# A hybrid decoder step: where the old states of the recurrent stage are scaled, who takes the first convolution tap, how masks and gates are formed

## The chip, the cores and the metric

The kernel runs on one core of a Trainium2 chip. A core has five engines that run their own instruction streams: TensorE (PE, matmuls; its weight loads are PEld), VectorE (DVE), ScalarE (ACT), GpSimd (POOL) and SyncE (SP, which issues DMAs here). They meet through semaphores. The metric is the device time of one execution in microseconds (us), lower is better.

## The reference

One layer of a decoder for 256 prompt tokens and 8 sequences of 8 sampled tokens (320 columns in all), width 2048. One projection feeds two branches. Branch A is a gated delta rule with 16 key heads and 32 value heads of 128 x 128 state; branch B is sparse attention. The part around the change:

```python
def causal_short_conv(x, buf, w):                       # 4 taps, then silu
    xp = jnp.concatenate([buf.astype(x.dtype), x], axis=1)
    y = sum(xp[:, i:i + L] * w[i] for i in range(CONV_W))
    return jax.nn.silu(y), xp[:, xp.shape[1] - (CONV_W - 1):]

decay = jnp.exp(jnp.where(incl, G[..., :, None] - G[..., None, :], -jnp.inf))
def chunk_step(s, xs):                                  # gated delta rule, one chunk
    u = u_c - jnp.einsum('bhck,bhkv->bhcv', w_c, s)
    o = jnp.einsum('bhck,bhkv->bhcv', qd_c, s) + jnp.einsum('bhij,bhjv->bhiv', qk_c, u)
    s = s * gt_c[..., None, None] + jnp.einsum('bhck,bhcv->bhkv', kt_c, u)

y = rms_norm(o, gdn_norm_g) * jax.nn.silu(z)            # the gates z
```

Everything is float32 at the edges.

## The kernel before

The big projections are a stream of weight blocks. Each unit is 1024 rows of 128 columns: SP loads it into `raw`, ACT rounds it into `whi`, DVE subtracts to get the rest `wlo` (the split), and PE multiplies both with the activations `xh`, `xl` into one of two PSUM banks `pm`: 8 pairs with `whi`, then 8 with `wlo`. `raw`, `whi` and `wlo` have three buffers each, so the split runs two units ahead.

All other work is written as Python generators ("sides") that are stepped between the pieces of the stream. A planner, the class `Clock`, keeps an estimated time for each engine from a cost formula (`cost`), and a side yields the time at which it wants to go on, for instance `self.ready(X)`. So the order of every engine's queue is fixed when the program is built; on the chip an instruction waits in that queue for what it needs. `force` steps sides until a buffer is free, whatever the planner's times.

The recurrent stage takes the projections of branch A, in eight groups of two key heads and four value heads (`gdn_chunks`). For each block of 128 channels `conv` copies the PSUM result to `xp` on ACT, forms four taps into the PSUM bank `u` (there is one such bank, a ring `cu`; rows name it ps), takes a tanh into `cth` on ACT, and DVE gates it into `kq`, `R` or `vf`. `z_done` forms the gates z (stored to `d_z`). `gb_gen` loads cumulated log decays into `gbt` (128 x 2 x 384), adds a mask of 0 and -1e30 and takes exponentials. `kq_gen` builds the matrices BT; `inverse` inverts them: 31 steps of two POOL instructions on `X` and `tmpx`, framed by DVE transposes of 32 x 32 blocks, then small matmuls that begin with `ps<-X,BD`. With the inverse XT in hand, `prompt_chain` and `sample_chain` run matmuls whose results DVE and ACT scale into `w` and `vt`. In `sample_chain`, S is the state of 8 sequences x 2 value heads (128 x 2048); its update S = S * gtr + k^T w reads four PSUM banks. `norm_gen` normalises the outputs `ot` (squares and their sums on ACT, `sc` holds the statistics, POOL takes the power -1/2), multiplies them with z and stores them to `d_ya`.

When all groups are through, the stream goes on with the remaining merge gates, `w_pb`, `w_pa` and `w_out`; `pb_open`, behind the second block of `w_pb`, first lets all normalisations end, and then loads gates (`sgb`).

Every instruction goes through the wrapper `Engine.__getattr__`, so the profile shows line L64 for all of them; groups are told apart by the names of their tiles.

Of the kernel before, what the change touches and what calls it, by code (L numbers as in the profile page):

```python
# [205 lines left out]
class Kernel:  # L206
# [260 lines left out]
    def consts(self):  # L467
        nc, f = self.nc, self.fix
        g, v = nc.gpsimd, nc.vector
        ji = self.l0.tile([128, 128], I32, name="ji")  # L470
# [8 lines left out]
        self.mask = self.l0.tile([128, 256], F32, name="mask")
        v.memset(self.mask, 0.0)  # L480
        self.select(self.mask)
        self.feat = f.tile([128, 81], F32, name="feat")
        self.gatp = f.tile([128, KB, 9], F32, name="gatp")

    def select(self, m):
        g = self.nc.gpsimd
# [2116 lines left out]
```

## Time and profile before

| | before |
|---|---|
| median of 3 runs | 2138.3 us (2138.07 to 2139.27) |
| profiled execution | 2140.89 us, its span 2139.2 us |
| mean granted TensorE clock | 0.994 |
| recurrent stage | about 728 to 1600 us of the span |
| HBM | 380.78 MB read, 42.65 MB written |

A row of groups reads: line, engine, operation, output <- inputs, shapes, xcount | busy us, mean ns of one | idle us of the engine before them <- who ended it. A row of the timeline reads: start, us, engine, line, operation, what, xcount, and in brackets the idle time before it and who ended that. PE's matmuls overlap, so the mean of one is longer than the step from one to the next.

### The profile page before, as it was taken

The page shows a single profiled execution, that of the slowest core. Times are in us where ns is not written, and L with a number is a line of the kernel's source. Part 1 is how long each engine was busy: PE and PEld are TensorE (multiplying, and loading weights), DVE is VectorE, ACT ScalarE, POOL GpSimd, SP SyncE. Part 2 cuts the span into 40 slices and gives each one's busy share as a digit, 9 for nine tenths or more (in the row PEclk, how much of TensorE's full clock was granted, in tenths as well). Part 3 has the DMA queues.
Part 4 walks back from the last instruction along what each step waited for, and adds up shares of the span by engine and source line. Part 5 has one row for each costly group of instructions (what it writes and reads, how often), then busy time and mean ns, then how long its engine had stood idle before and what let it go on. Part 6 is the DMA issues. An engine that isn't in the chain of part 4 may idle for free.

```text
span 2139.2 us, 44986 instructions
## 1 busy us (share of the span) xinstructions
PE 2093.5 (98%) x17741; PEld 2024.0 (95%) x17741; DVE 1462.1 (68%) x2881; ACT 1005.1 (47%) x2290; POOL 491.6 (23%) x713
## 2 busy tenths in 40 slices
PE   7999999999999999999999999999999999999997
PEld 7999999999999999898989998999999999999997
DVE  4776648899845577888778788778867445445443
ACT  4225443333434456565756565666556334233343
POOL 1001000000010128094636084508550000000000
PEclk9999999999999999999999999999999999999998
DMA  9996659885686757575757684758488767555562
GB/s 346 334 336 184 192 148 262 244 253 139 200 274 187 223 157 191 149 213 151 209 154 207 166 220 129 200 156 225 131 217 249 221 200 214 167 157 144 166 178 84
DMA packets 658595, 426.69 MB, mean 199 GB/s; under 512 B 19568, under 2 KB 642896, under 8 KB 656080
## 3 DMA queue, kind: packets, MB, share of 16 engines
q1 hardware_dynamic: 654304, 401.17, 65.8%
q0 software_dynamic: 3616, 21.02, 2.7%
q8 instruction: 139, 2.28, 0.4%
q10 hardware_dynamic: 464, 1.65, 0.2%
q14 instruction: 72, 0.59, 0.1%
HBM read 380.78 MB, written 42.65 MB: 198 GB/s over the span
## 4 chain that ended last, share of the span: by engine, by line
issue 24%; PE 19%; DVE 9%; POOL 5%; ACT 2%; DMA 1%; DVEq 0%; SPq 0%; POOLq 0%; ACTq 0%
PE pm L64 14%; PE ps L64 5%; POOL X L64 2%; POOL tmpx L64 2%; DVE wlo L64 2%; DVE S L64 2%; DVE ps L64 1%; DVE blk L64 1%; ACT ot L64 1%; POOL sc L64 1%; DVE X L64 0%; ACT whi L64 0%; DVE w L64 0%; DVE sc L64 0%; DVE BT L64 0%
## 5 line engine op out<-in xcount | busy, mean ns | idle before, releaser
L64 PE MATMUL pm<-xh,whi 128*128 128x320 f32 (+1 forms) x3108 | 942.1, 317 | 5.9 <-ACT whi L64 4.4
L64 PE MATMUL pm<-xl,whi 128*128 128x320 f32 (+1 forms) x3108 | 912.2, 308 | 0.4 <-DVE xl L64 0.3
L64 DVE TENSOR_TENSOR wlo<-raw,whi 128x1024 fp32r<-128x1024 f32 x466 | 580.3, 1254 | 247.2 <-ACT whi L64 225.9
L64 PEld LDWEIGHTS pm<-xh,whi 128*128 128x128 f32 x3108 | 586.4, 189 | 28.7 <-issue 18.0
L64 PEld LDWEIGHTS pm<-xl,whi 128*128 128x128 f32 x3108 | 586.8, 189 | 1.5 <-DVE xl L64 0.8
L64 ACT ACTIVATE whi<-raw 128x1024 fp32r<-128x1024 f32 x466 | 489.4, 1059 | 175.0 <-PE pm L64 115.8
L64 PE MATMUL pm<-xh,wlo 128*128 128x320 f32 (+1 forms) x3108 | 521.8, 307 | 3.6 <-DVE wlo L64 3.5
L64 PEld LDWEIGHTS pm<-xh,wlo 128*128 128x128 f32 x3108 | 469.2, 188 | 5.4 <-DVE wlo L64 5.3
L64 POOL TENSOR_TENSOR X<-X,tmpx 128x31 f32<-128x31 f32 (+15 forms) x248 | 180.6, 728 | 19.4
L64 POOL TENSOR_TENSOR tmpx<-blk,X 128x31 f32<-128x31 f32 (+15 forms) x248 | 168.9, 681 | 18.4
L64 DVE SCALAR_TENSOR_TENSOR ps<-xp,cs,ps 128x344 f32<-128x344 f32 x192 | 111.5, 581 | 6.8
L64 POOL TENSOR_TENSOR rfin<-rfin,mh 128x3 f32<-128x3 f32 x1 | 0.8, 848 | 485.9 <-DVE rfin L64 485.9
L64 PE MATMUL pm<-y1h,whi 128*128 128x320 f32 x336 | 99.2, 308 | 0.0
L64 PE MATMUL pm<-y1l,whi 128*128 128x320 f32 x336 | 99.1, 307 | 0.0
L64 POOL TENSOR_TENSOR sc<-sc,mh 128x6 f32<-128x6 f32 (+1 forms) x24 | 43.5, 1813 | 229.4 <-DVE sc L64 178.5
L64 POOL DMA_INDIRECT a<-in_cache_k_dram,idx x8 | 7.5, 937 | 283.1 <-PE ps L64 268.1
L64 DVE SCALAR_TENSOR_TENSOR S<-S,gtr,ps 128x128 f32<-128x128 f32 x256 | 67.5, 346 | 0.1
L64 ACT ACTIVATE xp<-pm 128x256 f32<-128x256 f32 (+1 forms) x128 | 32.0, 304 | 70.5 <-PE pm L64 70.5
L64 PE MATMUL ps<-xh,whi 128*128 128x320 f32 (+1 forms) x220 | 64.7, 309 | 0.0
L64 PE MATMUL ps<-xl,whi 128*128 128x320 f32 (+1 forms) x220 | 63.6, 304 | 0.0
L64 PEld LDWEIGHTS pm<-y1l,whi 128*128 128x128 f32 x336 | 63.1, 188 | 0.0
L64 PEld LDWEIGHTS pm<-y1h,whi 128*128 128x128 f32 x336 | 62.8, 187 | 0.0
(426 smaller groups left out, 2883.7 us busy)
## 6 DMA issues: line engine op xcount, KB each, us to landing
raw<-in_w_in_dram SPq DMA_DIRECT2D x328, 512.0 KB
raw<-in_w_pa_dram SPq DMA_DIRECT2D x64, 512.0 KB
rawx<-in_w_ada_dram SPq DMA_DIRECT2D x18, 1024.0 KB
a<-in_w_ada_dram SPq DMA_DIRECT2D x16, 1024.0 KB
S<-in_state_gdn_dram SPq DMA_DIRECT2D x32, 512.0 KB
out_dram<-S SPq DMA_DIRECT2D x32, 512.0 KB
raw<-in_w_pb_dram SPq DMA_DIRECT2D x32, 512.0 KB
raw<-in_w_out_dram SPq DMA_DIRECT2D x32, 512.0 KB
```

The source lines that it names most:

```text
L64: made = fn(*args, **kw)
```

## The change

Nine edits, all but the first three in the stage above:

- the planner's costs: a transpose of 3-dimensional pieces 0.2 + 0.0019 us an element (before, the general 0.16 + 0.00106), an `affine_select` 0.3 + 0.0009;
- the mask builder `select` is written into `consts`, and the stage's `mask3` goes;
- the four early gates (`z_early`) change as `z_done` does;
- conv: the first tap is an ACT copy with a scale;
- gates: z = (tanh + 1) * p in one DVE instruction straight from the bank; the factor `gh` is applied in `norm_gen`;
- decay masks: five `affine_select` on POOL for each key head in place of the DVE addition;
- inverse: the BD matmuls are placed 1.5 us after X is ready by the planner;
- chains: `w` for two heads in one instruction; S is scaled by POOL after its last read, and DVE adds one bank (512 elements) at a time;
- norm: two statistics steps merged, one on POOL; the scaling of `ot` is placed 1.5 us after its factors are ready by the planner.

```diff
@@ cost
+            if op == "transpose" and len(outs[0].ap) > 2:
+                return 0.2 + n * 0.0019
...
-        if op == "memset":
-            return 0.1 + n * 0.0009
+        if op in ("memset", "affine_select"):
+            return (0.1 if op == "memset" else 0.3) + n * 0.0009
@@ conv
-        self.ts(u[:, 0:344], xp[:, 0:344], wv(0), None, OP.mult)
+        self.act(u[:, 0:344], xp[:, 0:344], AF.Copy, scale=wv(0))
@@ z_done
-        self.force(lambda: self.zf.free and self.cth.free)
-        z, t = self.zf.get(), self.cth.get()
-        self.act(z, p[:, :NT], AF.Copy, scale=self.gh)
-        self.act(t[:, :NT], p[:, :NT], AF.Tanh, scale=0.5)
-        self.stt(z, t[:, :NT], 1.0, z, OP.add, OP.mult)
-        self.cth.put(t)
+        self.force(lambda: self.zf.free)
+        z = self.zf.get()
+        self.act(z, p[:, :NT], AF.Tanh, scale=0.5)
+        self.stt(z, z, 1.0, p[:, :NT], OP.add, OP.mult)
@@ gb_gen
-        self.tt(gb, gb, self.mask3.rearrange("p (o i) -> p o i", o=1).to_broadcast([128, 2, 384]), OP.add)
+        self.emitted += 1
+        g = gb[:, :, 0:256].rearrange("p v (t i) -> p v t i", t=2)
+        nc.gpsimd.affine_select(g, g, pattern=[[0, 2], [0, 2], [1, 128]], compare_op=OP.is_ge, fill=NEG, base=0,
+                                channel_multiplier=-1)
+        for v in range(2):
+            g = gb[:, v, 256:384].rearrange("p (b q) -> p b q", b=8)
+            nc.gpsimd.affine_select(g, g, pattern=[[-16, 8], [0, 16]], ...)
+            g = gb[:, v, 256:384].rearrange("p (b q t) -> p b q t", b=8, q=2)
+            nc.gpsimd.affine_select(g, g, pattern=[[16, 8], [0, 2], [1, 8]], ...)
@@ inverse, ahead of the BD matmuls
-        yield
+        yield self.ready(X) + 1.5
@@ prompt_chain (twice) and sample_chain
-        for v in range(2):
-            self.ts(wt[:, v, :], p[:, 128 * v:128 * v + 128], stl(v, 0), None, OP.mult)
+        self.tt(wt, p[:, 0:256].rearrange("p (v d) -> p v d", v=2), stl(0), OP.mult)
@@ sample_chain
         self.R.put(R)
+        self.tt(S, S, self.gtr[:, :, hv:hv + 2].rearrange("p b (v o) -> p b v o", o=1).to_broadcast([128, NB, 2, 128]),
+                OP.mult, eng=nc.gpsimd)
...
         yield
+        yield self.ready(S)
         yield from self.need(self.ps_side, 4)
...
         for j in range(4):
-            for pp in range(2):
-                for v in range(2):
-                    bb = 2 * j + pp
-                    self.stt(S[:, bb, v, :], S[:, bb, v, :], self.gtr[:, bb, hv + v:hv + v + 1],
-                             ps[j][:, 256 * pp + 128 * v:256 * pp + 128 * v + 128], OP.mult, OP.add)
+            sj = S[:, 2 * j:2 * j + 2].rearrange("p b v d -> p (b v d)")
+            self.tt(sj, ps[j], sj, OP.add)
@@ norm_gen
-        self.tt(mv(6), mv(6), qf, OP.mult)
-        self.ts(m[:, 6:12], m[:, 6:12], 1.0 / 128, EPS, OP.mult, OP.add)
+        self.stt(mv(6), mv(6), 1.0 / 128, qf, OP.mult, OP.mult)
+        self.ts(m[:, 6:12], m[:, 6:12], EPS, None, OP.add, eng=nc.gpsimd)
...
         self.tt(mv(12), mv(12), qf, OP.mult)
+        yield self.ready(m) + 1.5
         for t in range(3):
...
-            self.tt(y[:, 0:NP], p[:, 0:NP], z[:, 0:NP], OP.mult)
+            self.stt(y[:, 0:NP], p[:, 0:NP], self.gh, z[:, 0:NP], OP.mult, OP.mult)
```

Since the planner's times change, the order of all queues in the stage changes with them. Three places follow; a number behind a name is that of a buffer.

DVE, the third state update (h = 2, buffer S_7862). Before:

```order
L64 TENSOR_TENSOR wlo_82<-raw_75,whi_79 128x1024
L64 STREAM_TRANSPOSE blk<-X 128x32x32
L64 SCALAR_TENSOR_TENSOR vt_7851<-ps_71,neG,vt_7851 128x128 x2
L64 SCALAR_TENSOR_TENSOR vf_7831<-cth_7814,ps_68 128x256
L64 SCALAR_TENSOR_TENSOR vf_7831<-cth_7814,ps_68 128x8x8
L64 SCALAR_TENSOR_TENSOR S_7862<-S_7862,gtr,ps_70 128x128 x4
L64 SCALAR_TENSOR_TENSOR S_7862<-S_7862,gtr,ps_69 128x128 x4
L64 SCALAR_TENSOR_TENSOR S_7862<-S_7862,gtr,ps_67 128x128 x4
L64 SCALAR_TENSOR_TENSOR S_7862<-S_7862,gtr,ps_72 128x128 x4
L64 TENSOR_TENSOR wlo_83<-raw_75,whi_80 128x1024
```

Now on DVE (the buffer is S_7857, the conv bank u is ps_68):

```order
L64 TENSOR_TENSOR wlo_81<-raw_77,whi_78 128x1024
L64 SCALAR_TENSOR_TENSOR w_7850<-w_7850,gtp,ps_71 128x128 x2
L64 TENSOR_TENSOR ot_7856<-ps_71,ot_7856 128x256
L64 TENSOR_TENSOR S_7857<-ps_70,S_7857 128x512
L64 TENSOR_TENSOR S_7857<-ps_67,S_7857 128x512
L64 TENSOR_TENSOR S_7857<-ps_69,S_7857 128x512
L64 TENSOR_TENSOR S_7857<-ps_72,S_7857 128x512
L64 COPY ct_7812<-xp_7808 128x27
L64 SCALAR_TENSOR_TENSOR ps_68<-xp_7808,cs_95,ps_68 128x344 x3
```

and on POOL, where the same group's two scalings stand around the start of the next inverse (the memset and copies of X):

```order
L64 TENSOR_TENSOR X<-X,tmpx 128x31
L64 TENSOR_TENSOR sc_7862<-sc_7862,mh 128x10
L64 MEMSET X 32x4x32 x3
L64 COPY X<-X 32x4x32 x2
L64 COPY XT_7843<-blk 32x12x32 x2
L64 TENSOR_TENSOR S_7857<-S_7857,gtr 128x2048
L64 MEMSET X 128x640
L64 COPY X<-BT_7834 32x384 x2
L64 COPY BO<-BT_7834 64x256
L64 TENSOR_TENSOR S_7858<-S_7858,gtr 128x2048
```

Sixteen DVE instructions become four, and the multiplication is a POOL instruction behind the old inverse.

ACT, at the fifth normalisation. Before, its scaling `ot<-ot,sc` stands right behind a conv's copies and ahead of two weight copies:

```order
L64 ACTIVATE cth_7814<-ps_68 128x344
L64 ACTIVATE xp_7812<-pm_66 128x256
L64 ACTIVATE xp_7812<-pm_66 128x8x8
L64 ACTIVATE xp_7812<-cs_96 128x8x3
L64 ACTIVATE ot_7860<-ot_7860,sc_7867 128x128 x6
L64 ACTIVATE whi_79<-raw_75 128x1024
L64 ACTIVATE whi_80<-raw_75 128x1024
```

Now, with the tap behind the conv's copies (`ps_68<-xp,cs`), two weight copies behind the tap, and the scaling behind these:

```order
L64 ACTIVATE whi_80<-raw_75 128x1024
L64 ACTIVATE xp_7809<-pm_65 128x256
L64 ACTIVATE xp_7809<-pm_65 128x8x8
L64 ACTIVATE xp_7809<-cs_96 128x8x3
L64 ACTIVATE ps_68<-xp_7809,cs_96 128x344
L64 ACTIVATE whi_78<-raw_76 128x1024
L64 ACTIVATE whi_79<-raw_76 128x1024
L64 ACTIVATE cth_7810<-ps_68 128x344
L64 ACTIVATE ot_7855<-ot_7855,sc_7861 128x128 x6
```

DVE, where `w_pb` begins to be merged (`M<-pm,sgb`). Before, the last gates of the stage (`zf`) were over long before; the rows ahead of M were splits alone:

```order
L64 TENSOR_TENSOR wlo_81<-raw_76,whi_78 128x1024
L64 TENSOR_TENSOR wlo_82<-raw_76,whi_79 128x1024
L64 TENSOR_TENSOR wlo_83<-raw_77,whi_80 128x1024
L64 TENSOR_TENSOR wlo_81<-raw_77,whi_78 128x1024
L64 TENSOR_TENSOR M<-pm_66,sgb 128x320
L64 TENSOR_TENSOR M<-pm_65,sgb 128x320
```

Now the last four gates stand directly ahead of it:

```order
L64 TENSOR_TENSOR wlo_81<-raw_77,whi_78 128x1024
L64 SCALAR_TENSOR_TENSOR zf_7829<-ps_69,gh,zf_7829 128x256
L64 SCALAR_TENSOR_TENSOR zf_7829<-ps_69,gh,zf_7829 128x64
L64 SCALAR_TENSOR_TENSOR zf_7830<-ps_67,gh,zf_7830 128x256
L64 SCALAR_TENSOR_TENSOR zf_7830<-ps_67,gh,zf_7830 128x64
L64 TENSOR_TENSOR M<-pm_66,sgb 128x320
L64 TENSOR_TENSOR M<-pm_65,sgb 128x320
```

On PE the eight BD steps stand, counted in weight matmuls from the start, at 4236, 4860, 5304, 5844, 6528, 6960, 7632, 8016 before and at 4296, 4812, 5316, 5832, 6552, 7056, 7512, 8196 now; `w_pb` begins at 8448 in both.

More of the change, by code (lines that the diff above doesn't have):

```diff
@@ L480, in consts @@
         v.memset(self.mask, 0.0)
[L481 to L486, printed above, removed]
+        m = self.mask
         g.affine_select(m[:, 0:128], m[:, 0:128], pattern=[[1, 128]], compare_op=OP.is_ge, fill=NEG, base=0,
@@ L493, in select @@
                         channel_multiplier=-1)
+        self.feat = f.tile([128, 81], F32, name="feat")
+        self.gatp = f.tile([128, KB, 9], F32, name="gatp")
     def startup(self):
@@ L1319, in z_early @@
     def z_early(self, p, h):
-        self.force(lambda: len(self.t_r.free) >= 2)
-        z, t = self.t_r.get(), self.t_r.get()
-        self.act(z, p[:, :NT], AF.Copy, scale=self.gh)
-        self.act(t, p[:, :NT], AF.Tanh, scale=0.5)
-        self.stt(z, t, 1.0, z, OP.add, OP.mult)
-        self.t_r.put(t)
+        self.force(lambda: self.t_r.free)
+        z = self.t_r.get()
+        self.act(z, p[:, :NT], AF.Tanh, scale=0.5)
+        self.stt(z, z, 1.0, p[:, :NT], OP.add, OP.mult)
         self.store(self.d_z[h], z, self.t_r)
@@ L1707, in gdn_open @@
         self.cth = Ring([a.tile([128, 356], F32, name=f"cth{j}") for j in range(1)])
-        self.mask3 = a.tile([128, 384], F32, name="mask3")
         self.ct = Ring([a.tile([128, 4, 32], F32, name=f"ct{j}") for j in range(2)])
@@ L1729, in gdn_open @@
         self.sc = Ring([b.tile([128, 44], F32, name=f"sc{j}") for j in range(4)])
-        nc.vector.memset(self.mask3, 0.0)
-        self.select(self.mask3[:, 128:384])
-        nc.vector.tensor_copy(self.mask3[:, 0:128], self.mask3[:, 128:256])
         for r in (self.xp.free, ):
@@ L1890, in z_done @@
     def z_done(self, p, h):
-        self.force(lambda: self.zf.free and self.cth.free)
-        z, t = self.zf.get(), self.cth.get()
-        self.act(z, p[:, :NT], AF.Copy, scale=self.gh)
-        self.act(t[:, :NT], p[:, :NT], AF.Tanh, scale=0.5)
-        self.stt(z, t[:, :NT], 1.0, z, OP.add, OP.mult)
-        self.cth.put(t)
+        self.force(lambda: self.zf.free)
+        z = self.zf.get()
+        self.act(z, p[:, :NT], AF.Tanh, scale=0.5)
+        self.stt(z, z, 1.0, p[:, :NT], OP.add, OP.mult)
         self.store(self.d_z[h], z, self.zf)
@@ L1906, in gb_gen @@
         yield
-        self.tt(gb, gb, self.mask3.rearrange("p (o i) -> p o i", o=1).to_broadcast([128, 2, 384]), OP.add)
+        self.emitted += 1
[4 more added lines that the diff above has]
+            g = gb[:, v, 256:384].rearrange("p (b q) -> p b q", b=8)
+            nc.gpsimd.affine_select(g, g, pattern=[[-16, 8], [0, 16]], compare_op=OP.is_ge, fill=NEG, base=0,
+                                    channel_multiplier=1)
+            g = gb[:, v, 256:384].rearrange("p (b q t) -> p b q t", b=8, q=2)
+            nc.gpsimd.affine_select(g, g, pattern=[[16, 8], [0, 2], [1, 8]], compare_op=OP.is_ge, fill=NEG, base=0,
+                                    channel_multiplier=-1)
         yield
@@ L2134, in scal @@
         c = (38, 10)[e]
-        stl = lambda v, t: sst[:, c + 3 * v + t:c + 1 + 3 * v + t]
+        stl = lambda t: sst[:, c + t:c + 4 + t:3].rearrange("p (v o) -> p v o", o=1).to_broadcast([128, 2, 128])
         return s, stl
@@ L2219, in prompt_chain @@
             self.act(x1[:, v, :], p[:, 128 * v:128 * v + 128], AF.Copy, scale=s(v, 1))
-        for v in range(2):
-            self.ts(wt[:, v, :], p[:, 128 * v:128 * v + 128], stl(v, 1), None, OP.mult)
+        self.tt(wt, p[:, 0:256].rearrange("p (v d) -> p v d", v=2), stl(1), OP.mult)
         self.ps_side.put(p)
@@ L2282, in sample_chain @@
         self.act(ot[:, 2], p[:, 0:256].rearrange("p (v d) -> p v d", v=2))
-        for v in range(2):
-            self.ts(wt[:, v, :], p[:, 128 * v:128 * v + 128], stl(v, 2), None, OP.mult)
+        self.tt(wt, p[:, 0:256].rearrange("p (v d) -> p v d", v=2), stl(2), OP.mult)
         self.ps_side.put(p)
@@ L2293, in sample_chain @@
         for j in range(4):
-            for pp in range(2):
-                for v in range(2):
-                    bb = 2 * j + pp
-                    self.stt(S[:, bb, v, :], S[:, bb, v, :], self.gtr[:, bb, hv + v:hv + v + 1],
-                             ps[j][:, 256 * pp + 128 * v:256 * pp + 128 * v + 128], OP.mult, OP.add)
+            sj = S[:, 2 * j:2 * j + 2].rearrange("p b v d -> p (b v d)")
+            self.tt(sj, ps[j], sj, OP.add)
             self.ps_side.put(ps[j])
@@ L2352, in norm_gen @@
             z = y = zs[v]
-            self.tt(y[:, 0:NP], p[:, 0:NP], z[:, 0:NP], OP.mult)
-            self.tt(y[:, NP:NT].rearrange("p (b t) -> p b t", t=TS),
-                    p[:, NP:384].rearrange("p (b q t) -> p b q t", q=2, t=TS)[:, :, 1, :],
-                    z[:, NP:NT].rearrange("p (b t) -> p b t", t=TS), OP.mult)
+            self.stt(y[:, 0:NP], p[:, 0:NP], self.gh, z[:, 0:NP], OP.mult, OP.mult)
+            self.stt(y[:, NP:NT].rearrange("p (b t) -> p b t", t=TS),
+                     p[:, NP:384].rearrange("p (b q t) -> p b q t", q=2, t=TS)[:, :, 1, :], self.gh,
+                     z[:, NP:NT].rearrange("p (b t) -> p b t", t=TS), OP.mult, OP.mult)
             self.ps_side.put(p)
```

## The prediction

> **What bounds the kernel now.** I read the busy shares first, then a table of stretches, then who made PE wait in the recurrent stage, then the granted clock there.
>
> ```profile
> span 2139.2 us, 44986 instructions
> PE 2093.5 (98%) x17741; PEld 2024.0 (95%) x17741; DVE 1462.1 (68%) x2881; ACT 1005.1 (47%) x2290; POOL 491.6 (23%) x713
> ```
>
> The next rows are stretches: us, then the busy time of PE, PEld, DVE, ACT and POOL, then the granted clock. The first is the recurrent stage, the second all behind it up to the last slice.
>
> ```profile
> 728.00:1600.00 872.00, 851.82 (x6861) 817.10 (x6860) 692.96 (x1523) 520.93 (x1422) 444.67 (x636) 0.99 0.66 180
> 1600.00:2120.00 520.00, 520.00 (x3592) 516.76 (x3591) 265.38 (x389) 205.08 (x324) 3.07 (x2) 1.00 0.62 179
> ```
>
> PE is the bound. Behind the stage it never pauses; in the stage it lacks 872.00 - 851.82 = 20.2 us. The orders of the two programs hold the same 15,227 matmuls, 3,707 of them outside the weight stream, so the change takes no PE work away. It can only move these 20.2 us, and what hangs on them. Here is who ended them (us in total, times, longest):
>
> ```profile
> PE ps L64 <- DVE X L64: 7.0, 5, 2.8
> PE pm L64 <- ACT whi L64: 4.4, 3, 2.5
> PE pm L64 <- DVE wlo L64: 3.1, 3, 1.8
> PE ps L64 <- DVE S L64: 2.5, 6, 0.6
> PE ps L64 <- DVE sc L64: 1.2, 1, 1.2
> PE ps L64 <- DVE PT L64: 0.9, 1, 0.9
> PE ps L64 <- DVE w L64: 0.4, 1, 0.4
> ```
>
> These seven are 19.5 us. A second loss hangs on them: three times in the stage the granted clock (third last column) stands at about half.
>
> ```profile
> 895.70:899.30 3.60, 3.00 (x13) 2.91 (x13) 3.60 (x15) 1.94 (x7) 1.10 (x3) 0.53 0.12 35
> 1380.40:1383.90 3.50, 3.50 (x67) 3.11 (x67) 3.39 (x6) 3.28 (x15) 1.50 (x4) 0.51 0.02 5
> 1585.20:1592.10 6.90, 6.22 (x104) 5.79 (x105) 3.63 (x6) 2.91 (x6) 2.56 (x7) 0.51 0.94 260
> ```
>
> PE's busy time there, at the missing share of the clock, costs 0.47 x 3.00 + 0.49 x 3.50 + 0.49 x 6.22 = 6.2 us. So the most that the change can bring is 20.2 + 6.2 = 26.4 us.
>
> **The change, part by part.** *The planner's transpose cost and the later X.* The last wait on X, the longest, reads so:
>
> ```profile
> 1581.40 0.25 POOL L64 TENSOR_TENSOR X<-X,tmpx 128x31 f32<-128x31 f32 x1
> 1581.68 2.01 DVE L64 STREAM_TRANSPOSE blk<-X 128x1024 f32<-128x1024 f32 x1 [3.00 <-POOL X L64]
> 1583.73 2.01 DVE L64 STREAM_TRANSPOSE X<-X 128x1024 f32<-128x1024 f32 x1
> 1585.63 1.18 DVE L64 TENSOR_TENSOR wlo<-raw,whi 128x1024 fp32r<-128x1024 f32 x1
> 1585.88 1.07 PE L64 MATMUL ps<-X,BD 32*32 32x32 f32 x32 [2.76 <-DVE X L64]
> ```
>
> The planner placed the BD matmuls as if a transpose took 0.16 + 1024 x 0.00106 = 1.25 us; it takes 2.01. The new cost is 2.15, and the yield adds 1.5: against the real pair PE now comes 2 x 0.90 + 1.5 = 3.3 us later. That is over the longest wait of 2.76, so the X waits (7.0) and the one of 1.2 put down to sc, which is also a BD matmul, go: 8.2, of which I keep 0.5. Weight matmuls cover the delay.
>
> *The normalisation.* Its ScalarE scaling now stands behind a yield. Without that, this happens (ACT, DVE, PE and POOL rows):
>
> ```profile
> 1108.57 0.23 ACT L64 ACTIVATE xp<-cs 128x24 f32<-128x24 f32 x1
> 1112.28 0.54 DVE L64 SCALAR_TENSOR_TENSOR vf<-cth,ps 128x256 f32<-128x256 f32 x2
> 1115.54 1.86 ACT L64 ACTIVATE ot<-ot,sc 128x128 f32<-128x128 f32 x6 [6.73 <-DVE sc L64]
> 1117.30 1.99 ACT L64 ACTIVATE whi<-raw 128x1024 fp32r<-128x1024 f32 x2
> 1118.12 0.56 POOL L64 TENSOR_TENSOR tmpx<-blk,X 128x220 f32<-128x220 f32 x1
> 1118.37 1.39 DVE L64 TENSOR_TENSOR wlo<-raw,whi 128x1024 fp32r<-128x1024 f32 x1 [2.87 <-ACT whi L64]
> 1118.40 0.42 PE L64 MATMUL pm<-xh,whi 128*128 128x320 f32 x1 [2.54 <-ACT whi L64]
> 1118.77 1.49 POOL L64 TENSOR_TENSOR X<-X,tmpx 128x220 f32<-128x220 f32 x1
> ```
>
> ACT stands 6.73 us at the scaling, the weight copy whi queues behind it, and PE runs dry for 2.54 us. In the stage:
>
> ```profile
> ACT ot L64 <- DVE sc L64: 58.3, 14, 7.9
> ACT cth L64 <- DVE ps L64: 42.6, 26, 3.6
> ```
>
> With the yield most of the 58.3 goes, and with it the three whi waits (4.4). The wlo waits (3.1) are DVE's backlog. Of these 7.5 us I take 5.5 as gone.
>
> *DVE's load.* These groups are cut or added to:
>
> ```profile
> L64 DVE SCALAR_TENSOR_TENSOR S<-S,gtr,ps 128x128 f32<-128x128 f32 x256 | 67.5, 346 | 0.1
> L64 DVE TENSOR_SCALAR ps<-xp,cs 128x344 f32<-128x344 f32 x64 | 36.9, 577 | 0.5
> L64 DVE TENSOR_SCALAR w<-ps,sc 128x128 f32<-128x128 f32 x96 | 28.5, 345 | 21.8 <-ACT ot L64 18.4 <-ACT vt L64 3.1
> L64 DVE TENSOR_TENSOR gbt<-gbt,mask 128x768 f32<-128x768 f32 x16 | 18.0, 1126 | 0.0
> L64 DVE SCALAR_TENSOR_TENSOR zf<-cth,zf 128x320 f32<-128x320 f32 x28 | 15.3, 547 | 22.1 <-ACT cth L64 22.0
> L64 DVE TENSOR_TENSOR PT<-ps,gbt 128x256 f32<-128x256 f32 x32 | 12.0, 416 | 0.0
> ```
>
> Out go 67.5 + 36.9 + 28.5 + 18.0 + 15.3 = 166 us. From PSUM, 256 elements cost 0.416 and 1024 in SBUF 1.18, so 1.0 ns an element: 0.67 for 512, 0.48 for 320. In come 64 x 0.67 + 48 x 0.416 + 28 x 0.48 = 76, and some 5 for gh as a scalar operand in 64 gates (a scalar operand is at most 0.08 each by the conv row: 0.577 against 0.416 + 88 x 0.001). DVE falls by 85 us, from 79% to 70% of the stage. The 3.8 us that PE waits for S, PT and w (2.5 + 0.9 + 0.4) shrink with it; the sixteen updates of one state end in 4 x 0.67 = 2.7 us in place of 16 x 67.5 / 256 = 4.2. I take 2.2 as gone.
>
> *ACT's load.*
>
> ```profile
> L64 ACT ACTIVATE zf<-pm,gh 128x320 f32<-128x320 f32 x28 | 14.8, 528 | 33.8 <-PE pm L64 33.7
> ```
>
> That copy goes (14.8 us), and 64 first taps come, of the same kind: 0.528 + 24 x 0.0008 = 0.55 each, 35 us. ACT goes from 60% to 62%. The price is not this but a wait: the tap writes the bank u that DVE's last gate of the conv before still reads, and whi queues behind the tap. Above, ACT was through with xp at 1108.80 and DVE with vf only at 1112.82: a tap would have stood 4.0 us. Bounds: nothing, if DVE keeps up, to the 42.6 us of the nearest row, cth behind ps, scaled to 64 taps, 105 us. PE paid 4.4 for ACT's 58.3, 0.075 a us, so 0 to 7.9; with a lighter DVE I take 1.0.
>
> *POOL's load.*
>
> ```profile
> L64 POOL TENSOR_TENSOR tmpx<-blk,X 128x256 f32<-128x256 f32 x8 | 5.0, 621 | 0.6
> L64 POOL TENSOR_TENSOR X<-X,tmpx 128x255 f32<-128x255 f32 x16 | 15.1, 943 | 1.3
> L64 POOL TENSOR_SCALAR_AFFINE_SELECT scp<-scp 128x256 f32<-128x256 f32 x2 | 0.8, 403 | 0.0
> ```
>
> A scaling of 2048 elements: from 0.25 (31) to 0.62 (256) the slope is 1.65 ns, which gives 3.6 us; by the mean that other work slows, 0.943, it is 3.1 ns and 6.5 us. I take 4.0, near the lower, because one long instruction meets others once. [...] Five selects a head at 0.4 to 0.9 are 2 to 4.5 us, 32 to 72 for 16 heads; the small tensor_scalar (16, under 0.3 each) fits beside. [...] The selects wait for a DMA that the mask addition never waited for (0.0 above). DVE's S update now waits for the scaling, with the split and the next conv behind it; but the planner holds it back until 0.25 + 2048 x 0.0028 = 6.0 us of scaling would be over, and 4.0 is less, so I cost that wait at nothing, and at up to 0.5 a state, 8 us, if the scaling takes its upper 6.5.
>
> What costs is what they do to DVE. In the rows at 1118 the split began 0.31 before POOL's instruction ended and took 1.39, not 1.18; and the next POOL instruction took 1.49, not some 0.6. Each waits for the other's end. A scaling of 4.0 then holds a split that falls into it by 2.0 on average, 32 us of DVE time over sixteen. The bounds for PE are 0 (DVE gets 85 us back) and 16 x 4.0 = 64 us. PE paid 3.1 us for all of DVE's wlo lateness so far, so I stay near the lower end: 2.0. [...]
>
> *The end.* The last inverse moves 180 weight matmuls later, so the last normalisation now ends where w_pb's second block does. There DVE already waits:
>
> ```profile
> 1686.79 0.89 DVE L64 TENSOR_TENSOR M<-pm,sgb 128x320 f32<-128x320 f32 x2 [5.01 <-DMA sgb<-d_sigb]
> ```
>
> Four gates (1.4 us) and two stores now stand ahead of that load, so the wait grows by 2 to 5 us. PE did not pause at 5.01; I take 0.5, bounds 0 to 3.
>
> *Clock.* The half-clock stretches follow clusters of waits, two of them BD waits. I take 4.0 of 6.2 as gone, bounds 0 and 6.2.
>
> *Sum:* 7.7 + 5.5 + 2.2 + 4.0 = 19.4 gone, 1.0 + 2.0 + 0.5 = 3.5 new: 15.9 less. The profiled execution took 2140.9 (its span and 1.7 around it), the median is 2138.3, 0.1% under it; I take 15.9 from the median: 2122.4.
>
> **The rivals.** *All of it.* Nothing new is paid and the clock stays whole: 2138.3 - 26.4 = 2112. For it: DVE 85 us lighter, and both corrections of the planner larger than the waits they meet. Against it: ACT and DVE keep dozens of waits for each other. *The taps take their share.* Their wait costs the upper 7.9 and the clock dips stay (4.0 more): 2122.4 + 6.9 + 4.0 = 2133. For it: the 4.0 us above. *No change.* The waits move: the order is new in the whole stage, and PE waits where steps are forced too early or a late engine is met. If three quarters of the 20.2 return elsewhere and the dips stay: 2133 plus some 4, 2137. *Slower, by the lock.* If DVE has no slack where the scalings run, PE pays most of each: 2.5 us, sixteen times, 40 in place of 2.0: 2160. It decides above (15.9 + 2.0 + 4.3) / 16 = 1.4 us a scaling. For it: the chain's own steps queue behind the blocked split. [...]
>
> **How the numbers follow.** A run tells about 0.2% from no change, 4.3 us: faster is below 2134.0, slower above 2142.6. Forecast, 2116 to 2129: 0.59. All of it, 2111 to 2116: 0.13. The taps, 2129 to 2134: 0.12. No change, up to 2142.6: 0.09. Slower: 0.07. So faster has 0.84. The range 2111 to 2133 holds the first two and four fifths of the third, 0.82; the forecast's own is 2116 to 2129.
>
> **What would show it.** PE busy in the stage nearer 872 for the same stretch; no row PE <- DVE X over 1 us; ACT ot <- DVE sc under 15 us; S updates near 0.67 x 64; a new row ACT ps <- DVE vf, kq or R, under 60 us; splits that begin in a scaling lasting up to 5 us; full clock in the stage. I am wrong if PE's waits in the stage stay over 15 us, if wlo becomes what PE waits for most, or if PE pauses by over 3 us where w_pb begins.

## The result, and the profile after

The changed kernel took 2117.47 us (median of 4 runs, 2115.83 to 2118.67), against 2138.26 (2138.07 to 2139.27) for the kernel before: a ratio of 0.9901, 95% interval 0.9884 to 0.9918, or 20.8 us less. 2122 was forecast, with 2116 to 2129 as the forecast's own range. The page of the changed kernel, its span and its busy time by engine:

```profile
span 2115.7 us, 44807 instructions
PE 2084.3 (99%) x17741; PEld 2021.2 (96%) x17741; DVE 1393.4 (66%) x2543; ACT 1028.8 (49%) x2322; POOL 594.5 (28%) x822
```

The stretches (us; busy time of PE, PEld, DVE, ACT, POOL; granted clock third from the right). The third row is the only half-clock stretch that is left in the stage:

```profile
728.00:1600.00 872.00, 866.73 (x6990) 837.08 (x6989) 632.64 (x1226) 552.41 (x1464) 533.88 (x731) 1.00 0.67 185
1600.00:2100.00 500.00, 500.00 (x3481) 496.47 (x3480) 256.41 (x348) 198.56 (x321) 12.01 (x6) 1.00 0.62 178
1335.10:1338.60 3.50, 3.50 (x15) 3.50 (x14) 0.18 (x1) 3.47 (x13) 3.03 (x6) 0.51 1.21 290
```

In the same 872 us PE lacks 5.3 us, not 20.2, and runs 129 more matmuls. Who made it wait there (us in total, times, longest):

```profile
PE ps L64 <- DVE vf L64: 3.3, 1, 3.3
PE ps L64 <- DMA cst<-in_conv_w_dram: 1.3, 1, 1.3
PE ps L64 <- DVE S L64: 0.4, 1, 0.4
PE ps L64 <- DVE w L64: 0.2, 1, 0.2
```

The rows for X, whi, wlo, sc and PT are gone. One wait is new, 3.3 us for v's transposes, and the half-clock stretch at 1335.1 follows it; the wait for the load of the convolution weights (cst) grew from 0.3 to 1.3. It comes about so (engine rows in order of time):

```profile
1331.62 1.04 ACT L64 ACTIVATE whi<-raw 128x1024 fp32r<-128x1024 f32 x1
1332.57 0.43 ACT L64 ACTIVATE cth<-ps 128x344 f32<-128x344 f32 x1
1332.69 1.30 DVE L64 TENSOR_TENSOR wlo<-raw,whi 128x1024 fp32r<-128x1024 f32 x1 [0.32 <-ACT whi L64]
1333.91 0.54 DVE L64 SCALAR_TENSOR_TENSOR vf<-cth,ps 128x256 f32<-128x256 f32 x2
1334.37 0.55 PE L64 MATMUL ps<-ident,vf 128*128 128x128 f32 x3 [3.31 <-DVE vf L64]
```

The last convolution's tanh (cth) queues on ACT behind a weight copy, and its gate (vf) on DVE behind a split. PE had been sent to the transposes 3.3 us too soon.

The moved work, in groups of the stage (busy us, mean ns, idle before):

```profile
L64 POOL TENSOR_TENSOR S<-S,gtr 128x2048 f32<-128x2048 f32 x14 | 51.2, 3654 | 93.7 <-issue 66.5 <-PE ps L64 21.3 <-DMA d_z<-zf 6.0
L64 POOL TENSOR_SCALAR_AFFINE_SELECT gbt<-gbt 128x128 f32<-128x128 f32 x64 | 33.6, 537 | 2.2
L64 DVE TENSOR_TENSOR wlo<-raw,whi 128x1024 fp32r<-128x1024 f32 x197 | 267.1, 1359 | 74.8 <-ACT whi L64 69.6 <-PE pm L64 3.4 <-DMA raw<-in_w_in_dram 0.9
L64 DVE TENSOR_TENSOR S<-ps,S 128x512 f32<-128x512 f32 x56 | 34.8, 685 | 1.3 <-PE ps L64 1.2
L64 ACT ACTIVATE ps<-xp,cs 128x344 f32<-128x344 f32 x64 | 35.3, 552 | 18.1 <-DVE ct L64 12.7 <-DVE R L64 3.5
L64 ACT ACTIVATE ot<-ot,sc 128x128 f32<-128x128 f32 x84 | 26.0, 391 | 1.3 <-DVE sc L64 1.3
```

ACT's wait for the normalisation's factors fell from 58.3 to 1.3 us. The split's mean of 1359 ns stands against 1300 in the same view of before.

### The profile page after: what moved, and what is told of

Read it like the earlier page. It is cut to its first block, busy times and chain, and to the rows that moved or that the text cites. A ratio compares the mean times of both kernels' runs of the same rounds, so it can differ in the third digit from the quotient of the medians.

```text
span 2115.7 us, 44807 instructions
## 1 busy us (share of the span) xinstructions
PE 2084.3 (99%) x17741; PEld 2021.2 (96%) x17741; DVE 1393.4 (66%) x2543; ACT 1028.8 (49%) x2322; POOL 594.5 (28%) x822
## 4 chain that ended last, share of the span: by engine, by line
PE 70%; issue 22%; DMA 3%; DVE 2%; ACT 1%; POOL 1%; SPq 1%; DVEq 0%; POOLq 0%; ACTq 0%
PE pm L64 55%; PE ps L64 15%; DMA raw<-in_w_ada_dram 1%; DMA rawx<-in_w_ada_dram 1%; SPq L64 1%; DMA out_dram<-S 1%; DVE wlo L64 1%; POOL X L64 0%; POOL tmpx L64 0%; ACT ps L64 0%; DMA out_dram<-sall 0%; ACT whi L64 0%; POOL sc L64 0%; DVE blk L64 0%; DVE S L64 0%
## 5 line engine op out<-in xcount | busy, mean ns | idle before, releaser
L64 PE MATMUL pm<-xh,whi 128*128 128x320 f32 (+1 forms) x3108 | 940.4, 317 | 1.2 <-DVE qiS L64 1.0
L64 PE MATMUL pm<-xl,whi 128*128 128x320 f32 (+1 forms) x3108 | 911.3, 308 | 0.4 <-DVE xl L64 0.3
L64 DVE TENSOR_TENSOR wlo<-raw,whi 128x1024 fp32r<-128x1024 f32 x466 | 596.2, 1286 | 261.7 <-ACT whi L64 244.4
L64 PEld LDWEIGHTS pm<-xh,whi 128*128 128x128 f32 x3108 | 585.4, 188 | 22.7 <-issue 17.6
L64 PEld LDWEIGHTS pm<-xl,whi 128*128 128x128 f32 x3108 | 586.4, 189 | 1.6 <-DVE xl L64 0.8
L64 ACT ACTIVATE whi<-raw 128x1024 fp32r<-128x1024 f32 x466 | 489.3, 1057 | 174.0 <-PE pm L64 109.3
L64 PE MATMUL pm<-xh,wlo 128*128 128x320 f32 (+1 forms) x3108 | 521.4, 307 | 0.5 <-DVE wlo L64 0.5
L64 PEld LDWEIGHTS pm<-xh,wlo 128*128 128x128 f32 x3108 | 469.4, 188 | 1.0 <-DVE wlo L64 1.0
L64 POOL TENSOR_TENSOR tmpx<-blk,X 128x31 f32<-128x31 f32 (+15 forms) x248 | 175.7, 708 | 17.6
L64 POOL TENSOR_TENSOR X<-X,tmpx 128x31 f32<-128x31 f32 (+15 forms) x248 | 167.5, 675 | 19.4
L64 DVE SCALAR_TENSOR_TENSOR ps<-xp,cs,ps 128x344 f32<-128x344 f32 x192 | 111.5, 581 | 32.6 <-ACT ps L64 28.0
L64 POOL TENSOR_TENSOR rfin<-rfin,mh 128x3 f32<-128x3 f32 x1 | 0.8, 849 | 457.5 <-DVE rfin L64 457.5
L64 PE MATMUL pm<-y1h,whi 128*128 128x320 f32 x336 | 99.4, 308 | 0.0
L64 PE MATMUL pm<-y1l,whi 128*128 128x320 f32 x336 | 99.2, 308 | 0.0
L64 POOL TENSOR_TENSOR S<-S,gtr 128x2048 f32<-128x2048 f32 x16 | 58.4, 3650 | 106.0 <-issue 78.1
L64 ACT ACTIVATE xp<-pm 128x256 f32<-128x256 f32 (+1 forms) x128 | 32.1, 303 | 113.0 <-PE pm L64 113.0
L64 POOL DMA_INDIRECT a<-in_cache_k_dram,idx x8 | 7.5, 936 | 280.2 <-PE ps L64 265.2
L64 PE MATMUL ps<-xh,whi 128*128 128x320 f32 (+1 forms) x220 | 64.7, 309 | 0.0
L64 PE MATMUL ps<-xl,whi 128*128 128x320 f32 (+1 forms) x220 | 63.7, 304 | 0.0
L64 PEld LDWEIGHTS pm<-y1l,whi 128*128 128x128 f32 x336 | 63.1, 188 | 0.0
L64 PEld LDWEIGHTS pm<-y1h,whi 128*128 128x128 f32 x336 | 63.0, 187 | 0.0
L64 ACT ACTIVATE vt<-ps,sc 128x128 f32<-128x128 f32 (+1 forms) x112 | 38.8, 408 | 44.4 <-PE ps L64 43.9
```

What stands on the lines that cost most here:

```text
L64: made = fn(*args, **kw)
```

## The experiments

Twelve kernels, in three groups, each group on one chip together with the kernel before. That kernel's median was 2140.95, 2142.7 and 2142.44 in these groups, so ratios are compared; their intervals are 2 to 4 us to either side. The quotient of the two medians differs from the ratio by up to 0.0006 (e9: 2115.33 / 2142.7 = 0.9872). "Gain" is (1 - ratio) x 2138.3. "By trace" is what the one profile gives from the weight matmul at which the stage begins (728.1 in before) to the end of the span, against before's 1411.1; it leaves out what comes before, where the traces differ by up to 6.6 (that matmul starts at 725.8 in e3 and at 732.4 in e9).

| kernel | ratio, 95% interval | gain, us | by trace, us |
|---|---|---|---|
| the changed kernel | 0.9901 (0.9884 to 0.9918) | 21.2 | 22.0 |
| e1: before, planner's edits alone | 0.9899 (0.9884 to 0.9914) | 21.6 | 22.0 |
| e2: after, planner's edits taken back | 0.9950 (0.9936 to 0.9963) | 10.7 | 10.8 |
| e3: after, tap on DVE | 0.9888 (0.9873 to 0.9903) | 23.9 | 22.4 |
| e4: after, S update on DVE | 0.9996 (0.9986 to 1.0005) | 0.9 | 3.8 |
| e5: after, S scaled twice | 1.0015 (1.0006 to 1.0024) | -3.2 | -5.5 |
| e7: before, transpose cost and later X alone | 0.9983 (0.9974 to 0.9992) | 3.6 | 3.6 |
| e8: before, later normalisation alone | 0.9924 (0.9911 to 0.9938) | 16.3 | 15.3 |
| e9: after, v's transposes later | 0.9866 (0.9851 to 0.9881) | 28.7 | 28.3 |
| e6: after's order, scaling in four pieces | 0.9909 (0.9893 to 0.9924) | 19.5 | 20.9 |
| e14: after's order, scaling twice | 0.9962 (0.9949 to 0.9976) | 8.1 | 10.0 |
| e13: after's order, S update on DVE | 0.9954 (0.9940 to 0.9968) | 9.8 | 7.7 |
| e11: e1, v's transposes later | 0.9894 (0.9879 to 0.9910) | 22.7 | 23.7 |

### e1 and e2: the planner's edits, and the moved work

e1 adds three edits to the kernel before; e2 takes the same three out of the changed kernel.

```diff
         if name == "vector":
+            if op == "transpose" and len(outs[0].ap) > 2:
+                return 0.2 + n * 0.0019
...
-        yield
+        yield self.ready(X) + 1.5
...
         self.tt(mv(12), mv(12), qf, OP.mult)
+        yield self.ready(m) + 1.5
```

> The kernel before with three planner edits alone: the transpose cost, the yield of 1.5 us after the inverse's X, the yield of 1.5 us ahead of the normalisation's scaling. Before is 2138.3, the changed kernel 2117.5, 20.8 apart. Theory P (the steps were placed too early): the X waits (7.0 + 1.2) and the whi waits (4.4) go and with them two of three half-clock stretches (about 4); S, PT, w and wlo waits (6.9) stay: 8.2 + 4.4 + 4 = 16.6 less, 2122. Theory D (VectorE was too loaded; its relief did it): PE stops waiting for X only as far as it now comes later, but wlo, S, PT, w grow with the load unchanged: at most half of the gain, 2128 to 2134.

> The changed kernel with those three planner edits taken back: only the work moved between VectorE, ScalarE and GpSimd is left (VectorE's busy time in the recurrent stage is then some 60 us under that of before). Theory P: X waits (about 7) and whi waits (about 4) come back and the clock dips with them: 2130 to 2134. Theory D: most of the gain stays, 2119 to 2124. If the two parts add up, this gain and that of the planner edits alone sum to 20.8; if both remove the same waits, each alone gives more than half of it.

e1 gained 21.6, as much as the whole change, with DVE as loaded as before (1461.5 us busy). That is more than theory P's 16.6, and theory D is out as an account of the whole. PE's waits in the stage, e1 first, then e2:

```profile
PE ps L64 <- DVE vf L64: 2.7, 1, 2.7
PE ps L64 <- DVE S L64: 1.3, 4, 0.3
PE ps L64 <- DVE w L64: 0.9, 4, 0.3
```

```profile
PE ps L64 <- DVE sc L64: 6.0, 2, 5.4
PE pm L64 <- ACT whi L64: 3.6, 2, 3.4
PE ps L64 <- DVE X L64: 2.2, 4, 0.9
PE ps L64 <- DVE w L64: 1.0, 1, 1.0
```

In e2 the BD matmuls wait as long as before (2.2 for X and 6.0 put down to sc, against 7.0 and 1.2), and of whi's 4.4 us 3.6 are back. Gone are the waits for wlo, S and PT, 6.5 us, and 3.4 us at half clock: the moved work alone is worth 10.7. The two gains make 32.3 and the whole change 21.2. They overlap: the planner's edits, too, end the waits for wlo and PT and half of those for S.

### e7 and e8: the planner's edits apart

e7 keeps the first two of the three edits above, e8 the third.

> The kernel before with the transpose cost and the yield after X alone (the normalisation as before). The three planner edits together gave 22 of the 21 of the whole change. Theory S (the waits are separate, each edit removes its own): the X waits and the one put down to sc go, 8.2, and with them the half-clock stretches near them, about 3: 11 under before; whi waits of about 4 stay. Rival O (any new order of this stage loses most waits by chance, so that either edit alone gives nearly all): 17 or more under before. Rival W (they only work together, since PE meets the next late engine): under 6.

> The kernel before with the yield of 1.5 us ahead of the normalisation's scaling alone. Theory S: the whi waits go (4.4), perhaps one half-clock stretch (1.7); the X waits stay: 5 to 7 under before. Rival O: 17 or more under. Rival W: under 3.

e7 gained 3.6, and rival W's line (under 6) holds; e8 gained 16.3, near rival O's (17). Theory S had the sizes the wrong way round. The main rows of PE's waits in the stage of e7, then of e8:

```profile
PE pm L64 <- DVE wlo L64: 4.8, 5, 1.8
PE ps L64 <- DVE vf L64: 2.7, 1, 2.7
PE pm L64 <- ACT whi L64: 2.1, 3, 0.9
PE ps L64 <- DVE X L64: 0.6, 2, 0.3
```

```profile
PE ps L64 <- DVE X L64: 4.6, 4, 1.9
PE ps L64 <- DVE S L64: 1.7, 5, 0.6
PE ps L64 <- DVE sc L64: 1.6, 1, 1.6
```

In e7 the X waits went as worked out (7.0 to 0.6, and the 1.2 for sc), but PE still waits 6.9 us for whi and wlo (7.5 before), 5.4 us are new (2.7 for vf, and 2.7 for two copies of the inverse that ACT makes behind the BD matmuls, X and blk), and the clock dipped four times (0.99 granted on average in the stage). In e8 the waits for whi and for wlo are gone, at a DVE load that is no lower (703 us in the stage, 693 before), and the X waits are smaller too. Apart they gain 19.9, together 21.6: within the intervals they add up.

Each of these edits also reorders the queues of the whole stage, and no run holds the order still for them. Rival O as it was put, that any new order gains nearly all, is out by e7, which has a new order too. How much of e8's 16.3 comes from its own order, and not from the later scaling, is open. By the rows 7.5 us are the waits for whi and wlo. Another 6.2 are smaller waits for X, sc and S (2.8) and 6.8 us at half clock in place of 13.7 (3.4); in before the half-clock stretches follow waits for PT, S and X, not for whi.

### e3: the tap

```diff
-        self.act(u[:, 0:344], xp[:, 0:344], AF.Copy, scale=wv(0))
+        self.ts(u[:, 0:344], xp[:, 0:344], wv(0), None, OP.mult)
```

> The changed kernel with the first tap of all 64 convolutions back on VectorE: ScalarE loses 35 us, VectorE gets 37 us. Theory D: VectorE's relief is worth something by its size; the net relief in the stage is 60 us, so 37 of it back returns about half of what the relief brought: 2120 to 2124. Theory P: VectorE still has over 20% free, so within 2 of the changed kernel, 2116 to 2120. Theory T (the tap's wait behind VectorE's last gates, 18 us on ScalarE, is paid by PE at 0.075 a us, 1.4): 2116.

0.9888 against 0.9901, intervals that overlap: the move of the tap is worth nothing that can be measured, neither by DVE's 37 us nor by ACT's wait. (e3, too, has an order of its own.)

### e4: the state update on DVE, in its own order

```diff
-        self.tt(S, S, self.gtr[...].to_broadcast([128, NB, 2, 128]), OP.mult, eng=nc.gpsimd)
...
-            sj = S[:, 2 * j:2 * j + 2].rearrange("p b v d -> p (b v d)")
-            self.tt(sj, ps[j], sj, OP.add)
+            for pp in range(2):
+                for v in range(2):
+                    bb = 2 * j + pp
+                    self.stt(S[:, bb, v, :], S[:, bb, v, :], self.gtr[:, bb, hv + v:hv + v + 1], ...)
```

> The changed kernel with the state update back to sixteen fused VectorE instructions of 128 elements, and no scaling of S on GpSimd: VectorE's busy time rises by about 67 - 35 = 32 us less the 17 us that eight splits lost in scalings. [...] Theory D: slower, since PE waits for S again (2.5 us before, 0.4 in the changed kernel): 2120 to 2122. Theory P: VectorE has room either way, 2116 to 2120.

Both theories missed: the whole gain was lost. In the stage, PE waited so, and the clock dipped four times (0.99 granted on average, 1.00 in the changed kernel):

```profile
PE ps L64 <- DVE vf L64: 7.9, 3, 2.7
PE ps L64 <- DVE S L64: 4.1, 12, 0.6
```

Yet e1 does the same update on DVE and gains 21.6. So it is not the update's cost alone; e4's order is one suspect, which e13 tries below.

### e5: the scaling doubled, in its own order

```diff
         self.tt(S, S, self.gtr[...].to_broadcast([128, NB, 2, 128]), OP.mult, eng=nc.gpsimd)
+        self.tt(S, S, self.gtr[...].to_broadcast([128, NB, 2, 128]), OP.mult, eng=nc.gpsimd)
```

> The changed kernel with GpSimd's scaling of each state done twice (so the states are scaled by the square of the decay): 16 more instructions of 3.6 us each, during which a split on VectorE is held up. In the changed kernel 8 of 15 splits near the 16 scalings began inside one and lost 17 us in all, and PE waited for a split 0.0 us in the stage. Theory N (VectorE has room for it): within 3 us of the changed kernel, which is 21 under before. Theory L (the hold is paid by PE): some 17 us more of lost VectorE time near the chain's steps gives 5 to 15 us, 6 to 16 under before.

24 us over the changed kernel, above both theories. The planner held each chain for both scalings, and PE met this, six times at an even distance of 111 us:

```profile
1106.12 7.31 POOL L64 TENSOR_TENSOR S<-S,gtr 128x2048 f32<-128x2048 f32 x2
1113.40 1.29 DVE L64 TENSOR_TENSOR S<-ps,S 128x512 f32<-128x512 f32 x2
1114.15 0.44 PE L64 MATMUL ps<-ident,vf 128*128 128x128 f32 x2 [1.02 <-DVE S L64]
```

DVE stands at the second scaling's end (1106.12 + 7.31 = 1113.43), four banks stay taken, and v's transposes wait for one. In this order the splits lost only 11.5 us in scalings (16.9 in the changed kernel), so held splits do not explain the loss; but the order and the second scaling were changed together, and e14 parts them.

### e6, e14, e13: three probes in the changed kernel's order

In these, the planner is told of the changed kernel's instructions while others are issued, so the rows of all queues keep their places. What is issued past the planner shows under its own line (L2272, L2301), not under L64. The core of e6:

```diff
-        self.tt(S, S, decay(0, NB), OP.mult, eng=nc.gpsimd)
+        for q in range(0, NB, 2):
+            nc.gpsimd.engine.tensor_tensor(S[:, q:q + 2], S[:, q:q + 2], decay(q, q + 2), OP.mult)
+        nc.gpsimd.enter("gpsimd", "tensor_tensor", (S, S, decay(0, NB), OP.mult), {})
```

> The changed kernel with each scaling of S cut into four GpSimd instructions of 512 elements, the planner told of the one long scaling, so that the order of all engines stays that of the changed kernel. A split that begins in a scaling then waits for the end of a quarter (up to 0.9 us) in place of up to 3.6. Theory N (VectorE's lost time is not paid by PE): VectorE gets back up to 12 of the 17 us and the time is that of the changed kernel within 2 (19 to 23 under before, ratio 0.989 to 0.991). Theory L (paid): 5 us or more faster than the changed kernel, 26 under before, ratio below 0.988.

0.9909, level with the changed kernel: PE pays nothing that can be measured for the splits' lost time, which fell from 16.9 to 9.0 us.

e14 has this in place of it:

```diff
+        for _ in range(2):
+            nc.gpsimd.engine.tensor_tensor(S, S, decay, OP.mult)
+        nc.gpsimd.enter("gpsimd", "tensor_tensor", (S, S, decay, OP.mult), {})
```

> The scaling done twice, as in the earlier run that was 3 slower than before, but with the planner told of one, so that the order is that of the changed kernel (states are scaled by the square of the decay). Theory R (the earlier loss came from the order: the planner held each chain 6 us longer): the time stays within 5 of the changed kernel, ratio 0.988 to 0.9925. [...]

0.9962: outside theory R's range, 13 us over the changed kernel and 11 under e5. So about half of e5's loss was order, and half is the second scaling itself. One way in which it reaches PE:

```profile
985.04 4.96 DVE L64 TENSOR_TENSOR wlo<-raw,whi 128x1024 fp32r<-128x1024 f32 x1
985.29 8.18 POOL L2272 TENSOR_TENSOR S<-S,gtr 128x2048 f32<-128x2048 f32 x2
989.91 2.04 DVE L64 STREAM_TRANSPOSE blk<-X 128x1024 f32<-128x1024 f32 x1
991.86 0.39 DVE L64 TENSOR_TENSOR w<-ps,sc 128x256 f32<-128x256 f32 x1
992.30 0.70 PE L64 MATMUL ps<-w,ktok 128*128 128x256 f32 x2 [2.35 <-DVE w L64]
```

The split is held for the first scaling, w queues behind it, PE waits 2.35 us. At 1190 even an addition of 6 elements was held: the two in the row took 3.22 us, where the median of the same addition in the changed kernel is 0.165:

```profile
1185.12 8.31 POOL L2272 TENSOR_TENSOR S<-S,gtr 128x2048 f32<-128x2048 f32 x2
1190.42 3.22 DVE L64 TENSOR_TENSOR sc<-sc 128x6 f32<-128x6 f32 x2
```

DVE's queue then ran on without a pause, and at 1196.37 PE had waited 1.50 us for `ot`. In all, 14 splits lost 24.4 us in scalings. But POOL, 62 us busier, is late itself as well: the waits for its X, sc and gbt grew by 5 us. How the 13 us divide between the held DVE instructions and POOL's lateness is not parted.

e13 issues no scaling and sixteen fused updates, and tells the planner of the scaling and four bank updates:

```diff
+        nc.gpsimd.enter("gpsimd", "tensor_tensor", (S, S, self.gtr[...], OP.mult), {})
...
+            nc.vector.engine.scalar_tensor_tensor(S[:, bb, v, :], S[:, bb, v, :], self.gtr[...], ps[j][...], op0=OP.mult, op1=OP.add)
...
+            nc.vector.enter("vector", "tensor_tensor", (sj, ps[j], sj, OP.add), {})
```

> The state update back to sixteen fused VectorE instructions and no scaling on GpSimd, as in the earlier run that gained nothing over before, but with the planner told of the scaling and the four bank updates, so that the order is that of the changed kernel. Theory R (that run lost by its order: three waits for vf and three half-clock stretches): within 4 of the changed kernel, ratio 0.989 to 0.992. Theory D (sixteen instructions of 4.2 us in place of 2.7, with four PSUM banks held that long, make PE wait): 10 or more over the changed kernel, ratio 0.995 or more.

0.9954: 11 us over the changed kernel, on theory D's side; so for this order the lighter update is worth 11. Of e4's 20, then, 11 is the heavier update and 9 its order. PE's main waits in e13 from 728 to 1700, where the clock dipped three times (0.99 granted on average in the stage) and not once:

```profile
PE ps L64 <- DVE S L2301: 3.3, 8, 0.8
PE ps L64 <- DVE vf L64: 2.6, 2, 2.4
PE ps L64 <- DMA cst<-in_conv_w_dram: 2.1, 1, 2.1
```

Here, then, an order made for four short updates lost by sixteen long ones. Why the planner, which knew e4's instructions, made a bad order for them and a good one for e1's is open.

### e9 and e11: v's transposes later

```diff
-        yield self.ready(self.V[hv], self.V[hv + 1], G["sst"])
+        yield self.ready(self.V[hv], self.V[hv + 1], G["sst"]) + 3.5
```

> The changed kernel with the transposes of v placed 3.5 us later on the planner's clock. They wait once for vf (3.3 us) in the changed kernel, and a half-clock stretch (3.4 us, costs 1.7) follows. Theory P (what is left is also a step placed too early): both go, 5 under the changed kernel, 26 under before. Rival M (the wait moves to the next step): within 2 of the changed kernel, 19 to 23 under before. Rival C (the chain is then too late and forced at the end): slower than the changed kernel by 2 or more.

> The kernel before with the planner's edits alone (transpose cost, later X, later normalisation) and v's transposes 3.5 us later; no work moved between engines. The planner's edits alone gave a ratio of 0.990, the changed kernel with later transposes 0.987. Theory P (moving the work is worth nothing once the steps stand late enough): 0.986 to 0.988, level with the latter. Theory D (VectorE, 69% busy in place of 66%, still makes PE wait for S and w, 2.2 us, and for what the later v brings): 0.989 to 0.992.

e9 is the best version: 0.9866, by the medians 27.4 us under before on its chip, against theory P's 26. Its whole list of waits in the stage:

```profile
PE ps L64 <- DMA cst<-in_conv_w_dram: 0.9, 1, 0.9
PE ps L64 <- ACT w L64: 0.5, 1, 0.5
PE ps L64 <- DVE vt L64: 0.4, 1, 0.4
```

No half-clock stretch is left there. e11, without any moved work, gained 22.7, on theory D's side: its waits sum to 2.0 us, but one half-clock stretch of 6.8 us (costs 3.4) stayed. With v's transposes later, the moved work is worth some 6 us by the ratios, whose intervals just touch, and 4.6 by trace.

## Why the prediction came out right, step by step

*The sum.* Both pages count 17741 matmuls (the prediction's 15,227 are counted in the programs' orders); that the change takes none away holds. 15.9 less was forecast, 20.8 came; 23.4 was gone of what was listed (19.4 forecast) and 4.3 was new (3.3 for vf and 1.0 more for cst; 3.5 forecast, for other things). That makes 19.1; by trace the part from the stage on gained 22.0, and the 2.9 between them is not assigned. That the sum came so near is in part luck: it adds terms that the experiments show to overlap, the planner's terms were too small and DVE's brought nothing beside them, and what was new had not been foreseen.

*BD waits: 7.7 gone.* In the changed kernel all 8.2 are. But alone the term is worth less than half of itself: in e7 the X waits are away, and 3.6 is gained, with 5.4 us of other waits new and one more half-clock stretch. Weight matmuls did cover the delay at the BD step, as the prediction has it; that nothing else would then be late held only with the normalisation moved as well.

*whi and wlo: 5.5 gone.* All 7.5 are. This term was too small: the later normalisation alone gave 16.3 in e8, 7.5 of it in these waits. "The wlo waits are DVE's backlog" was half of it, as the longest of them in before shows (ACT, DVE and PE rows):

```profile
1216.92 1.87 ACT L64 ACTIVATE ot<-ot,sc 128x128 f32<-128x128 f32 x6 [3.13 <-DVE sc L64]
1219.76 1.23 DVE L64 TENSOR_TENSOR wlo<-raw,whi 128x1024 fp32r<-128x1024 f32 x1 [2.88 <-ACT whi L64]
1230.10 2.31 DVE L64 TENSOR_TENSOR wlo<-raw,whi 128x1024 fp32r<-128x1024 f32 x2
1231.33 1.44 PE L64 MATMUL pm<-xh,wlo 128*128 128x320 f32 x8 [1.83 <-DVE wlo L64]
```

DVE worked without a pause (state update, convolution, transpose) from 1219.76 to the split that PE waits for, so there was a backlog. But it had begun 2.88 us late, for a whi that stood behind the normalisation's scaling on ACT. In e8, without that, no wlo wait is left at DVE's old load.

*S, PT, w: 2.2 gone.* 3.2 (0.6 left). DVE fell by 1462.1 - 1393.4 = 69 us, not 85; the splits took 15 us more (584.3 before, 599.1 after, all 466). Its single durations came as worked out: 0.685 for 512 elements (0.67 forecast), 0.419 for w, 0.483 for the gate. What was not seen is how this term stands to the others: on top of the planner's edits it brought nothing (0.9899 alone, 0.9901 with), without them 10.7.

*Clock: 4.0 gone.* Three stretches became one: 6.2 - 1.7 = 4.5.

*The tap: 1.0.* PE paid nothing, and e3 shows none. ACT waited 12.7 + 3.5 us at taps, far under the bound of 105.

*Held splits: 2.0.* As at 1118 in before, splits that began in a POOL instruction lasted past its end. The longest:

```profile
1496.63 3.62 POOL L64 TENSOR_TENSOR S<-S,gtr 128x2048 f32<-128x2048 f32 x1 [5.64 <-PE ps L64]
1497.15 4.17 DVE L64 TENSOR_TENSOR wlo<-raw,whi 128x1024 fp32r<-128x1024 f32 x1
```

It began 0.52 after the scaling, and 3.62 - 0.52 + 1.08 = 4.18. The 1.08 is what a split took after POOL's end in the trace of before. Eight splits fell into a scaling and lost 16.9 us (32 forecast); all ended 1.08 or 1.09 after it, while `w` and `vt` from PSUM took in scalings the 0.42 and 0.34 that they take elsewhere; PE's row for wlo is gone, and e6 shows no price that can be measured. The rival "slower, by the lock", in which PE pays for held splits, was not empty: e14's second scaling cost 13 / 16 = 0.8 us a state, held DVE instructions and POOL's lateness together. Nor were splits alone held: in e14 two additions of 6 elements on `sc` took 3.22 us. A scaling took 3.65 us (4.0 forecast), the five selects 4 x 0.537 + 0.750 = 2.9 a head (2 to 4.5 forecast), and POOL came to 533.88 of 872, 61% (444.67, 51%, in before).

*The end: 0.5.* The sgb wait did not grow by 2 to 5 but shrank from 5.01 to 4.29, and PE did not pause. That step failed, at no cost:

```profile
1665.75 0.89 DVE L64 TENSOR_TENSOR M<-pm,sgb 128x320 f32<-128x320 f32 x2 [4.29 <-DMA sgb<-d_sigb]
```

*Not in the sum:* the wait for vf (3.3). Before, it was not there; it appears as soon as the inverse comes later (e1, e7). The prediction covered the delay with weight matmuls and did not ask what would be late next; that was v. Nor did the rival "all of it" bound the gain: its ceiling of 26.4 was for the waits and the clock of before, and e9, 27.4 under before by the medians and 28.3 by trace, is level with it or a little past it.

## What to carry to other kernels

Where PE is the bound and an order is planned, first ask whether a wait is a step placed too early: giving the planner a measured duration, and two waiting steps some slack, gained 21.6 us here, while moving 69 us of work off VectorE gained 10.7 alone and nothing on top. Remove waits together and look for the next late producer, since one removed alone (e7) lets PE run into the next; and test moved work in a fixed order as well as in its own, since a new order was worth 9 to 11 us by itself (e4 against e13, e5 against e14). The planner's own edits were not tested so, and a part of their 21.6 may be such an order.

## What the hardware showed

The half-clock stretches lie on a grid. In all fourteen traces (before, after, twelve experiments), leaving out the two ends of the span, they last 3.41 or 6.83 us, and where a trace has several, their starts are whole multiples of 3.413 us apart (142 and 202 of them in before; 4, 101 and 166 in e4). Cut PE's time on that grid, between 300 us and the last slices: 13 windows had 2.0 us or more of idle PE, and all 13 were followed by a half-clock stretch; of 33 with 1 to 2 us it was 9, of some 90 with 0.3 to 1 us it was 4. Ahead of the stretch at 1585.3 in before PE was idle for 2.13 us of the window, ahead of that at 1335.1 in the changed kernel for 2.65. The clock granted in them is 0.50 (before and after), so a stretch of 3.41 us costs PE some 1.7 us. A long wait alone does not bring one: of the 18 single waits of over 2.0 us 14 were followed by one, and the other 4 are waits that a border of the grid divides, so that neither window has 2 us, such as e14's 2.35 us at 992.3 (1.09 and 1.26 us in two windows) and the 2.54 us in before at 1118 (1.78 and 0.8). In these traces, then, what counts is how much of a wait falls into one window, though that is not all: below 2 us 13 windows are followed by a stretch and some 110 are not.
